# Gate weights two rows to a partition in four wide slots, down weights in four small ones

## Chip, cores and metric

The kernel runs on 1 core of a Trainium2 chip. The metric is the device time of one execution in microseconds, lower is better; the median of three runs is given. One further execution was taken by the profiler; its rows carry the readings below.

## What is computed

The reference is `second_block(first_block(x))` for 512 tokens of width 1024 in fp32. The first block is a gated convolution beside a linear recurrence, the second an attention layer (two kinds of heads) and a mixture of experts. The change touches the mixture of experts, which takes most of the time:

```python
def _moe_sequence(h, w_router, b_router, w_gate_up, b_gate_up, w_down, b_down):
    logits = (jnp.einsum('ld,de->le', h, w_router) + b_router).astype(jnp.float32)
    top_val, top_idx = lax.top_k(logits, TOP_K)
    gates = jax.nn.softmax(top_val, axis=-1).astype(h.dtype)
    ...
    xs = h[tok] 
    hgu = lax.ragged_dot(xs, w_gate_up, group_sizes) + b_gate_up[e_sorted]
    act = _clamped_swiglu(hgu)
    out = lax.ragged_dot(act, w_down, group_sizes) + b_down[e_sorted]
    out = out * gates.reshape(-1)[order][:, None]
    return jax.ops.segment_sum(out, tok, num_segments=L)
```

`w_gate_up` of one expert is 1024 x 2048 (8 MB), `w_down` 1024 x 1024 (4 MB). All 32 experts' weights are read once, 384 MB.

## The kernel before

The experts run as 32 passes, in the order of how many tokens chose them. A pass takes the expert's tokens in groups ("items") of up to 128; passes 3 and 9 (PAIRS) have two items, every other one has one, and what goes beyond is done by `further_tiles` (L1997). Weights come in pieces of 1 MB. `units(b)` (L298) lists what pass b consumes: 8 gate pieces of its own expert (128 rows of 2048 columns, one row to a partition, 8192 bytes) and then 4 down pieces of the expert before it (256 rows of 1024 columns; two neighbouring rows to a partition, 8192 bytes, or in the passes of PAIRS and TINY two rows 128 apart, 4096 bytes each).

The pieces go through `class Weights` (L89 to L160). `add` (L100) appends to a list of work, `issue` (L108) takes the next piece and the first free slot and starts one DMA on SyncE's queue (SP, L115), `release` (L148) gives a slot back and issues the next piece, and `get` hands the next piece over in order. There are 12 slots of 1 MB: 2 from the start (L221), 7 added at L1349, 3 at L2051. A DMA is issued at the moment in the program in which a slot is freed, so its place in SP's queue and the wait for the slot's last reader are set by that.

How a piece is used depends on the pass. In the passes called SMALL (1, 2, the even ones and the last six; few tokens) TensorE takes the piece in fp32 as it is (`small_products`, matmuls L1903, bias L1897), and the slot is released behind the piece's last matmul. In the others ScalarE and VectorE split it into a high and a low part (L140, L141), the slot is released there, and TensorE makes three products (L1921 for gates, L1932 for downs). In PAIRS the slot is kept until the second item has been through.

Beside the products of a pass, `beside(b)` lays out what prepares the next ones, by the index of the unit: ahead of unit 4 GpSimd gathers the rows of the next expert's tokens from DRAM (`rows_of`, an indirect DMA, L1569, on the software queue q0; weights are on q1), behind unit 9 TensorE transposes them (`transposed_rows` L1643 for small items of 64 or 32 rows, `transposed` L1648 for 128 rows), so that the contracted dimension lies on the partitions. The activations of the way down are transposed in `act_T` (L1673), which in passes with paired down rows reads every second column. A pass ends with a scatter that adds its rows to the result in DRAM (L1665, also on q0). Behind the last down piece stand the further tiles and the final layer norm (L2069 to L2160), which take four freed slots as scratch (`keep`).

Of the kernel before, what the change touches and what calls it, by code (L numbers as in the profile page):

```python
# [9 lines left out]
F32 = mybir.dt.float32  # L10
# [8 lines left out]
D = 1024  # L19
# [70 lines left out]
class Weights:  # L90
# [1 line left out]


    def __init__(self, nc, pools, slots):
        self.nc, self.slots = nc, list(slots)
# [4 lines left out]
    def add(self, *loads, split=True, n=2048, pieces=1, late=0):  # L100

        self.todo.append((loads, split, n, pieces, self.last + late))
        self.last += 1

    def ready(self):
        return self.raw and self.raw[0][-1] == self.used

    def issue(self):  # L108
        if not self.todo:
            return  # L110
        loads, split, n, pieces, at = self.todo.pop(0)
        pool, tag = slot = self.slots.pop(0)
        t = pool.tile([128, 2048], F32, tag=tag, name="wraw", bufs=1)
        for view, src in loads:
            self.nc.sync.dma_start(out=view(t), in_=src() if callable(src) else src)  # L115
        self.raw.append((t, split, n, pieces, slot, at))
        self.raw.sort(key=lambda r: r[-1])

    def prefetch(self):
        while self.slots and self.todo:  # L120
            self.issue()

    def split(self):
        t, s, n, pieces, slot, _ = self.raw.pop(0)
        self.used += 1
        if not s:
            self.part.append((t, slot))
            return
        raw = (t, slot)
        if s != "both":  # L130
            self.slots.append(slot)
        pool, tag = slot = self.parts.pop(0)
        self.parts.append(slot)
        hi = pool.tile([128, 2048], F32R, tag=tag + "h", name="whi", bufs=1)
        lo = pool.tile([128, 2048], F32R, tag=tag + "l", name="wlo", bufs=1)
        self.part.append((hi, lo, *raw) if s == "both" else (hi, lo))

        def piece(i):
            c = slice(n * i // pieces, n * (i + 1) // pieces)
            self.nc.scalar.copy(out=hi[:, c], in_=t[:, c])  # L140
            self.nc.vector.tensor_tensor(out=lo[:, c], in0=t[:, c], in1=hi[:, c].bitcast(F32), op=OP.subtract)  # L141
            if i == pieces - 1 and s != "both":
                self.issue()

        piece(0)
        self.rest = [lambda i=i: piece(i) for i in range(1, pieces)]

    def release(self, slot):  # L148
        self.slots.append(slot)
        self.issue()  # L150

    def ahead(self, n):
        while len(self.part) < n and self.ready():
# [15 lines left out]
def block_kernel(ctx, tc, A, out, dbg=None, upto=99):  # L169
# [48 lines left out]
        return t  # L218


    RAW, RAWK, RAWX = 2, 7, 3  # L221
    W = Weights(nc, wp, [(wp, f"wraw{i}") for i in range(RAW)])

    def flat(t):
        return t
# [60 lines left out]

    PASSES, ni = [], 0
    for p in range(NE):  # L290
        k = 1 + (p in PAIRS)
# [12 lines left out]
    def paired(p):  # L304

        return p not in PAIRS and p not in TINY

    def rows2(w, pairs):
        return w.rearrange("(p k) n -> p k n" if pairs else "(k p) n -> p k n", p=128)

    def add_unit(p, dn, u, of, late=0):
        def src():
            w = of(p)[dn]
            return rows2(w[256 * u:256 * u + 256, :], paired(p)) if dn else w[128 * u:128 * u + 128, :]
        W.add((kn(2, 1024) if dn else flat, src), split="both" if p in PAIRS else p not in SMALL,
              late=late)

    def add_block(b, of):
        for p, dn, u in units(b):
# [1026 lines left out]
    v_ = A["b_router_2"]  # L1346
    sp.dma_start(out=rb, in_=bass.AP(tensor=v_.tensor, offset=v_.offset, ap=[[0, 128], [1, NE]]))
    W.parts.insert(0, (pK, "wpart2"))
    W.slots += [(pK, f"wraw{RAW + i}") for i in range(RAWK)]  # L1349
    W.prefetch()  # L1350
    l1b = bcast(A["ln1_b_2"], pC, "l1b")
    xg2 = [pK.tile([128, D], F32, name=f"xg{i}") for i in range(2)]
# [269 lines left out]
    def pick(onehot_e, kt):  # L1622
# [373 lines left out]

    def further_tiles():  # L1997

        at_slot, slots = W.slots[0], W.slots[1:]
        total = nc.values_load(xt_i[0:1, NX:NX + 1], min_val=0, max_val=NX)  # L2000
        msch.close()
        with tc.For_i(0, total, 1) as it:  # L2002
            with tc.manual_schedule():
# [23 lines left out]
                for g, (w, src) in enumerate(((gu[:, 0:D], xT), (gu[:, D:], xT), (dn, aT))):  # L2027
                    p_ = [psa("pg") for _ in range(2)]
                    add_bias(p_, se, g, bias_p.bitcast(F32))
                    for q_ in range(4):  # L2030
                        wpool, tag = slots[nl % len(slots)]
                        nl += 1
                        t = wpool.tile([128, 2, 1024], F32, tag=tag, name="wl", bufs=1)
                        sp.dma_start(out=t, in_=rows2(w[256 * q_:256 * q_ + 256, :], g == 2))
                        for k in range(2):
                            for c in range(2):
                                pe.matmul(p_[c], src[:, 2 * q_ + k, :], t[:, k, 512 * c:512 * c + 512],
                                          start=False, stop=(q_ == 3 and k == 1))
                    if g < 2:
                        ac = pM.tile([128, 512], F32, tag="ac", name="ac", bufs=2)  # L2040
                        for c in range(2):
                            swiglu(p_[c].unsqueeze(1), ac[:, 256 * c:256 * c + 256], 1)
                        for c in range(2):
                            act.copy(out=aT[:, 4 * g + 2 * c:4 * g + 2 * c + 2, :], in_=act_T(ac, c))
                    else:
                        for c in range(2):
# [19 lines left out]
    for b in range(NE + 1):  # L2066
        before, midst = beside(b)
        for j, (p, dn, u) in enumerate(units(b)):
            j += 8 * (b == NE)  # L2069
            last = b == NE and u == 3  # L2070
            if last:
                keep = [slot for slot in W.slots if slot[0] is not pM][:4]
                for slot in keep:
                    W.slots.remove(slot)
                oT = keep[1][0].tile([128, 16, 128], F32R, tag=keep[1][1], name="oT", bufs=1)
                for i in range(4):
                    dve.tensor_scalar(out=oT[:, i, :], in0=iotab, scalar1=its[NI - 1]["tk"][:, i:i + 1], scalar2=None,
                                      op0=OP.is_equal)
                hx = []
                for p_, tag in keep[2:]:  # L2080
                    t = p_.tile([128, 2, D], F32, tag=tag, name="hx", bufs=1)
                    hx += [t[:, 0, :], t[:, 1, :]]
                l2 = keep[0][0].tile([128, 2, D], F32, tag=keep[0][1], name="l2", bufs=1)
                for k, v in enumerate((A["ln2_g_2"], A["ln2_b_2"])):
                    sp.dma_start(out=l2[:, k, :], in_=bass.AP(tensor=v.tensor, offset=v.offset, ap=[[0, 128], [1, D]]))
            run(before[j])
            if b == NE and u == 0:
                run([(finish, n) for n in PASSES[NE - 2]])
            if last:
                further_tiles()  # L2090
                for i in range(4):
                    sp.dma_start(out=hx[i], in_=acc_d[128 * i:128 * i + 128, :])
            ahead = AHEAD - (b == NE)
            w = W.get(ahead - 1)
            if len(PASSES[p]) > 1:
                n0, n1 = PASSES[p]
                products(n0, dn, u, w, lambda: None)
                run(midst[j])
                products(n1, dn, u, w, lambda: None)
            else:  # L2100
                products(PASSES[p][0], dn, u, w, lambda: run(midst[j]))
            if ahead > 1:
                W.beyond(3)
            else:
                W.ahead(ahead)
            if b == 0:
                next(ordering, None)
            elif b > 1:
                next(lists, None)
        if b == 0:  # L2110
            run(before[8])
# [75 lines left out]
```

## Time and profile before

| | |
|---|---|
| median of 3 runs | 1892.73 us (1892.15 to 1892.87) |
| profiled execution | 1887.72 us |
| its span | 1885.8 us, mean granted TensorE clock 0.962 |
| TensorE busy | 1701.9 us (90%) |
| VectorE, ScalarE, GpSimd busy | 1118.5, 751.9, 516.0 us |
| SP's DMA queue (q1) | 115568 packets, 475.24 MB, 63.7% of 16 engines over the span |
| GpSimd's DMA queue (q0) | 11024 packets, 25.39 MB, 4.9% |
| gate pieces | 256 DMAs of 1 MB, median 20.4 us from issue to landing |
| down pieces | 128 DMAs of 1 MB, median 21.5 us |

The span is the time between the first and the last instruction in the trace, the profiled execution's own time is the whole of it. Busy shares are averages over a kernel with unlike stages: the mixture of experts runs from about 809 to 1853 us of the span, and there the DMA engines are full most of the time. A line of a time slice or window gives each engine's busy time, TensorE's granted clock (1.00 is 2.4 GHz, 0.50 is 1.2 GHz) and the share of the 16 DMA engines; the share can read slightly above 1. In a timeline row the bracket at the end tells how long the engine was idle before it, and what ended that.

### The profile page before, as it was taken

What the parts mean: (1) busy time and instruction counts of PE and PEld (TensorE: products, weight loads), DVE (VectorE), ACT (ScalarE), POOL (GpSimd) and SP (SyncE); (2) the same over time, 40 slices, a digit from 0 to 9 for tenths busy, and PEclk for the clock granted to TensorE, in tenths of its full rate; (3) what the DMA queues carried; (4) which work ended last, traced back from release to release, by engine and by line L of the source; (5) the groups of instructions that cost most, each with busy time, mean ns of one, the idle gap of its engine ahead of it and who ended that gap; (6) DMA issues with size and microseconds to landing.
All of it is one profiled execution on the core that took longest, in us unless ns stands there. A gap on an engine that the chain in (4) does not pass through costs nothing. (4 is left out here: it accounts for less than half of the span.)

```text
span 1885.8 us, 23223 instructions
## 1 busy us (share of the span) xinstructions
PE 1701.9 (90%) x8713; PEld 1111.8 (59%) x8713; DVE 1118.5 (59%) x1425; ACT 751.9 (40%) x894; POOL 516.0 (27%) x400
## 2 busy tenths in 40 slices
PE   4899785979998899978999999999999999999885
PEld 3687664758787677854565565566446545642221
DVE  6799983785746555756665566557547645731013
ACT  5323532742335545332364344445435533520001
POOL 3899994550311221311121101111110101110102
PEclk8999897989999899989999999999999999999997
DMA  8322221336131003769999999999999999999993
GB/s 301 90 73 73 78 90 45 112 135 213 59 104 56 1 1 110 298 265 365 390 395 412 399 413 398 403 403 411 420 402 406 404 404 396 403 406 396 406 414 132
DMA packets 127442, 503.51 MB, mean 267 GB/s; under 512 B 15226, under 2 KB 57784, under 8 KB 79712
## 3 DMA queue, kind: packets, MB, share of 16 engines
q1 hardware_dynamic: 115568, 475.24, 63.7%
q0 software_dynamic: 11024, 25.39, 4.9%
q8 instruction: 69, 1.13, 0.2%
q10 hardware_dynamic: 736, 1.38, 0.2%
q14 instruction: 45, 0.37, 0.1%
HBM read 488.55 MB, written 19.84 MB: 270 GB/s over the span
## 5 line engine op out<-in xcount | busy, mean ns | idle before, releaser
L141 DVE TENSOR_TENSOR wlo<-wraw,whi 128x2048 fp32r<-128x2048 f32 (+1 forms) x201 | 457.0, 2282 | 152.9 <-ACT whi L140 146.7
L140 ACT CAST whi<-wraw 128x2048 fp32r<-128x2048 f32 (+1 forms) x201 | 379.6, 1891 | 193.6 <-DMA wraw<-w_down 73.8
L1903 PE MATMUL pg<-wraw,xTs 128*64 128x512 f32 (+1 forms) x1664 | 274.6, 516 | 12.0 <-DMA wraw<-w_gate_up 12.0
L1903 PEld LDWEIGHTS pg<-wraw,xTs 128*64 128x64 f32 (+1 forms) x1664 | 85.5, 126 | 169.1 <-issue 120.7
L1903 PE MATMUL pg<-wraw,ats 128*64 128x512 f32 (+1 forms) x832 | 145.0, 524 | 6.3 <-DMA wraw<-w_down 3.8
L1658 DVE TENSOR_SCALAR lp<-pg 128x512 f32<-128x512 f32 (+1 forms) x47 | 31.1, 662 | 198.4 <-ACT sg L1657 196.8
L1665 POOL DMA_INDIRECT acc_d<-y,back x20 | 34.2, 1711 | 381.4 <-ACT y L1875 363.9
L561 POOL TENSOR_TENSOR acc<-acc,sparel 128x512 f32<-128x512 f32 x91 | 133.3, 1464 | 7.7 <-ACT acc L550 0.2
L1569 POOL DMA_INDIRECT xg<-h_d,ix x34 | 53.8, 1583 | 247.2 <-PE pg L1903 115.9
L1921 PE MATMUL pg<-whi,xTh 128*128 128x512 f32 x416 | 116.2, 401 | 0.4 <-issue 0.4
L1921 PE MATMUL pg<-whi,xTl 128*128 128x512 f32 x416 | 114.8, 398 | 0.0
L1921 PE MATMUL pg<-wlo,xTh 128*128 128x512 f32 x416 | 113.2, 394 | 0.0
L1665 POOL DMA_INDIRECT acc_d<-y,ix x13 | 28.8, 2219 | 288.3 <-ACT y L1878 206.9
L554 DVE SCALAR_TENSOR_TENSOR pc<-v,C,pc 128x512 f32<-128x512 f32 x144 | 101.6, 748 | 2.1 <-ACT pc L550 0.9
L1657 ACT ACTIVATE sg<-pg 128x512 f32<-128x512 f32 (+1 forms) x47 | 25.7, 573 | 184.3 <-PE pg L1903 101.1
L559 POOL TENSOR_SCALAR sparel<-v,C 128x512 f32<-128x512 f32 x91 | 93.8, 1031 | 14.0 <-DVE V L476 5.4
L1921 PEld LDWEIGHTS pg<-whi,xTh 128*128 128x128 f32 x416 | 75.9, 188 | 26.0 <-issue 10.6
L1921 PEld LDWEIGHTS pg<-wlo,xTh 128*128 128x128 f32 x416 | 78.7, 189 | 17.7
L1903 PEld LDWEIGHTS pg<-wraw,ats 128*64 128x64 f32 (+1 forms) x832 | 40.8, 126 | 80.9 <-issue 52.4
L1921 PEld LDWEIGHTS pg<-whi,xTl 128*128 128x128 f32 x416 | 76.6, 188 | 16.3
L1932 PE MATMUL pg<-wlo,ath 128*128 128x512 f32 x208 | 67.9, 408 | 10.3 <-DVE wlo L141 10.3
L213 DVE TENSOR_TENSOR atl<-pat,ath 128x256 fp32r<-128x256 f32 x52 | 20.0, 421 | 92.4 <-ACT ath L212 92.4
(660 smaller groups left out, 3349.7 us busy)
## 6 DMA issues: line engine op xcount, KB each, us to landing
wraw<-w_gate_up SPq DMA_DIRECT2D x256, 1024.0 KB, 20.4
wraw<-w_down SPq DMA_DIRECT2D x128, 1024.0 KB, 21.5
wraw<-w_in SPq DMA_DIRECT2D x17, 1024.0 KB, 5.1
wraw<-w_out SPq DMA_DIRECT2D x8, 1024.0 KB, 4.9
mraw<-mod_w SPq DMA_DIRECT2D x7, 1024.0 KB, 15.4
wraw<-w_in SPq DMA_DIRECT2D x14, 512.0 KB, 4.1
wraw<-pw_w SPq DMA_DIRECT2D x4, 1024.0 KB, 5.1
wraw<-mod_w SPq DMA_DIRECT2D x4, 1024.0 KB, 5.1
```

The lines of the kernel that those rows point to most:

```text
L140: self.nc.scalar.copy(out=hi[:, c], in_=t[:, c])
L141: self.nc.vector.tensor_tensor(out=lo[:, c], in0=t[:, c], in1=hi[:, c].bitcast(F32), op=OP.subtract)
L554: dve.scalar_tensor_tensor(out=acc[:, c, :] if j == 29 and not np_ else st_["o"], in0=v[:, j:j + S], scalar=dw_col(j, c), in1=st_["o"], op ...
L559: pool.tensor_scalar(out=pr_, in0=v[:, j:j + S], scalar1=dw_col(j, c), scalar2=0.0, op0=OP.mult, op1=OP.add)
L561: pool.tensor_tensor(out=acc[:, c, :], in0=acc[:, c, :], in1=pr_, op=OP.add)
L1569: pool.indirect_dma_start(out=xg, out_offset=None, in_=h1_d[:, :], in_offset=bass.IndirectOffsetOnAxis(ap=ix[0:w], axis=0), bounds_check=S ...
L1657: act.activation(out=sg, in_=v2[:, :, :, 0], func=AF.Sigmoid, scale=1.702)
L1658: dve.tensor_scalar(out=lp, in0=v2[:, :, :, 1], scalar1=-6.0, scalar2=8.0, op0=OP.max, op1=OP.min)
L1665: pool.indirect_dma_start(out=dst, out_offset=bass.IndirectOffsetOnAxis(ap=ix, axis=0), in_=y, in_offset=None, bounds_check=nt * S - 1, oo ...
L1903: pe.matmul(o, l, t[:, c0:c0 + n_], start=False, stop=u == 3 and k == 1 if dn else u == 7)
L1921: pe.matmul(it["acc"][c // 2][:, c % 2, :], l, r[:, 512 * c:512 * c + 512], start=False, stop=u == 7 and j == 2)
L1932: pe.matmul(it["acc"][2][:, c, :], l, r[:, c0:c0 + 512], start=False, stop=end)
```

## The change

Gate units are added two at a time: one DMA of 2 MB brings 256 rows, rows 2p and 2p+1 of the block next to each other on partition p (16384 contiguous bytes). A list of slots for each size takes the place of the one list: four small slots of 1 MB (two from the start, one at L1349, one at L2051) serve the down pieces and all earlier weights, four wide slots of 2 MB (three at L1349, one at L2051) the gate pairs. The total is 12 MB as before. A wide slot carries two units, and only the second one gives it back; a released slot issues the next piece of its own size. The row order on the partitions makes unit 2i the even and unit 2i+1 the odd rows of a block, so the transpositions of the gathered tokens take every other column (`every_other`). The scratch of the tail is three wide slots in place of four, and `further_tiles` reads its down weights as neighbouring rows.

```diff
+    def add(self, *loads, split=True, n=2048, pieces=1, late=0, size=1):
+
+        self.todo.append((loads, split, n, pieces, self.last + late, size))
+        self.last += size
 
...
-    def issue(self):
-        if not self.todo:
-            return
-        loads, split, n, pieces, at = self.todo.pop(0)
-        pool, tag = slot = self.slots.pop(0)
-        t = pool.tile([128, 2048], F32, tag=tag, name="wraw", bufs=1)
+    def issue(self, *sizes):
+
+        for i, (loads, split, n, pieces, at, size) in enumerate(self.todo):
+            if size in sizes and self.slots[size]:
+                break
+        else:
+            return False
+        self.todo.pop(i)
+        pool, tag, _ = slot = self.slots[size].pop(0)
+        t = pool.tile([128, 2048 * size], F32, tag=tag, name="wraw", bufs=1)
         for view, src in loads:
             self.nc.sync.dma_start(out=view(t), in_=src() if callable(src) else src)
-        self.raw.append((t, split, n, pieces, slot, at))
+        for k in range(size):
+            self.raw.append((t[:, 2048 * k:2048 * k + 2048] if size > 1 else t, split, n, pieces,
+                             slot if k == size - 1 else (), at + k))
         self.raw.sort(key=lambda r: r[-1])
+        return True
 
     def prefetch(self):
-        while self.slots and self.todo:
-            self.issue()
+        while self.issue(1, 2):
+            pass
 
...
             if i == pieces - 1 and s != "both":
-                self.issue()
+                self.release(slot)
 
         piece(0)
         self.rest = [lambda i=i: piece(i) for i in range(1, pieces)]
 
     def release(self, slot):
-        self.slots.append(slot)
-        self.issue()
+        if slot:
+            self.slots[slot[2]].append(slot)
+            self.issue(slot[2])
 
...
         def src():
             w = of(p)[dn]
-            return rows2(w[256 * u:256 * u + 256, :], paired(p)) if dn else w[128 * u:128 * u + 128, :]
-        W.add((kn(2, 1024) if dn else flat, src), split="both" if p in PAIRS else p not in SMALL,
-              late=late)
+            if dn:
+                return rows2(w[256 * u:256 * u + 256, :], paired(p))
+            return w[128 * u:128 * u + 256, :].rearrange("(p k) n -> p (k n)", p=128)
+        if dn or u % 2 == 0:
+            W.add((kn(2, 1024) if dn else flat, src), split="both" if p in PAIRS else p not in SMALL,
+                  late=late, size=1 if dn else 2)
 
...
-    W.slots += [(pK, f"wraw{RAW + i}") for i in range(RAWK)]
+    W.slots[1].append((pK, "wraw2", 1))
+    W.slots[2] += [(pK, f"wide{i}", 2) for i in range(3)]
...
+    def every_other(k):
+
+        k0 = 256 * (k // 2)
+        return slice(k0 + k % 2, k0 + 256, 2)
+
     def transposed_rows(xg):
         w = xg.shape[0]
         pt = psa("pxt")
         for k in range(8):
-            pe.transpose(pt[:, w * k:w * k + w], xg[:, 128 * k:128 * k + 128], ident[0:w, 0:w])
+            pe.transpose(pt[:, w * k:w * k + w], xg[:, every_other(k)], ident[0:w, 0:w])
         return pt[:, 0:8 * w].rearrange("p (k n) -> p k n", k=8)
 
     def transposed(xg, a, pt):
         for k in range(4):
-            pe.transpose(pt[:, 128 * k:128 * k + 128], xg[:, 512 * a + 128 * k:512 * a + 128 * k + 128], ident)
+            pe.transpose(pt[:, 128 * k:128 * k + 128], xg[:, every_other(4 * a + k)], ident)
         return slice(4 * a, 4 * a + 4), pt.rearrange("p (k n) -> p k n", k=4)
 
...
-    W.slots += [(pM, f"wraw{RAW + RAWK + i}") for i in range(RAWX)]
+    W.slots[1].append((pM, "wraw3", 1))
+    W.slots[2].append((pM, "wide3", 2))
...
-                keep = [slot for slot in W.slots if slot[0] is not pM][:4]
+                keep = [slot for slot in W.slots[2] if slot[0] is not pM]
                 for slot in keep:
-                    W.slots.remove(slot)
-                oT = keep[1][0].tile([128, 16, 128], F32R, tag=keep[1][1], name="oT", bufs=1)
+                    W.slots[2].remove(slot)
+                oT = keep[0][0].tile([128, 16, 128], F32R, tag=keep[0][1], name="oT", bufs=1)
+                l2 = keep[2][0].tile([128, 2, D], F32, tag=keep[2][1], name="l2", bufs=1)
```

## Rows read from the trace of the kernel before

**Rows 1.** Windows: busy PE, PEld, DVE, ACT, POOL; PE clock, DMA share, GB/s.
```profile
950.00:1000.00 50.00, 49.86 (x382) 34.94 (x372) 34.16 (x31) 27.89 (x24) 8.45 (x4) 1.00 1.02 393
1750.00:1800.00 50.00, 42.47 (x190) 12.07 (x188) 3.68 (x13) 3.36 (x7) 3.72 (x4) 1.00 1.02 405
```
**Rows 2.** Waits of TensorE's weight loads, 1750 to 1850: total us, times, longest.
```profile
PEld pg L1903 <- DMA wraw<-w_gate_up: 22.6, 16, 3.0
```
**Rows 3.** The weight DMA issued at 939.7: issue ns, and us to landing.
```profile
L115 SPq DMA_DIRECT2D wraw<-w_down x1: 383/383/383, 939.7 to 939.7; - x1
DMA to landing us min/median/max: 5.0/5.0/5.0
```
**Rows 4.** The weight DMA issued at 1133.2, the same view.
```profile
L115 SPq DMA_DIRECT2D wraw<-w_gate_up x1: 333/333/333, 1133.2 to 1133.2; - x1
DMA to landing us min/median/max: 8.9/8.9/8.9
```
**Rows 5.** DMA in 877 to 880: packets; queue: packets, MB, share of 16.
```profile
DMA packets 331, 1.27 MB, mean 423 GB/s; under 512 B 21, under 2 KB 21, under 8 KB 331
q1 hardware_dynamic: 331, 1.27, 103.1%
```
**Rows 6.** DMA in 1197.5 to 1200, the same view.
```profile
DMA packets 147, 1.07 MB, mean 429 GB/s; under 512 B 16, under 2 KB 16, under 8 KB 16
q1 hardware_dynamic: 147, 1.07, 101.6%
```
**Rows 7.** All 34 gathers of L1569, from issue to landing.
```profile
DMA to landing us min/median/max: 3.4/9.0/11.4
```
**Rows 8.** DMA queues in 1017.5 to 1020, while a gather's rows move.
```profile
q1 hardware_dynamic: 102, 0.76, 72.1%
q0 software_dynamic: 97, 0.32, 31.1%
```
**Rows 9.** Timeline of TensorE: start, us, transposition, [idle before and what ended it].
```profile
843.35 0.68 PE L1643 MATMUL pxt<-sq,xg 32*128 32x32 f32 x8 [2.52 <-DMA xg<-h_d,ix]
865.49 0.68 PE L1643 MATMUL pxt<-sq,xg 64*128 64x64 f32 x8 [1.62 <-DMA xg<-h_d,ix]
895.40 0.82 PE L1648 MATMUL pxt<-sq,xg 128*128 128x128 f32 x5 [2.94 <-DMA xg<-h_d,ix]
...
964.12 1.03 PE L1648 MATMUL pxt<-sq,xg 128*128 128x128 f32 x8
999.34 0.71 PE L1643 MATMUL pxt<-sq,xg 64*128 64x64 f32 x8
1025.49 1.03 PE L1648 MATMUL pxt<-sq,xg 128*128 128x128 f32 x8
```
**Rows 10.** The gather issued at 953.2.
```profile
L1569 POOL DMA_INDIRECT xg<-h_d,ix x1: 1056/1056/1056, 953.2 to 953.2; - x1
DMA to landing us min/median/max: 9.6/9.6/9.6
```
**Rows 11.** The gather issued at 988.7.
```profile
L1569 POOL DMA_INDIRECT xg<-h_d,ix x1: 1904/1904/1904, 988.7 to 988.7; - x1
DMA to landing us min/median/max: 10.3/10.3/10.3
```
**Rows 12.** The gather issued at 1013.1.
```profile
L1569 POOL DMA_INDIRECT xg<-h_d,ix x1: 1063/1063/1063, 1013.1 to 1013.1; - x1
DMA to landing us min/median/max: 8.7/8.7/8.7
```
**Rows 13.** Windows behind two of these idle times, columns as in rows 1.
```profile
895.90:899.30 3.40, 3.40 (x28) 1.80 (x26) 3.40 (x5) 2.97 (x3) 0.00 (x0) 0.50 1.01 405
865.00:866.00 1.00, 0.51 (x8) 0.54 (x8) 1.00 (x1) 0.00 (x0) 0.00 (x0) 1.00 0.99 418
```
**Rows 14.** Weight loads of the transpositions: ns min/median/max, first and last start.
```profile
L1673 PEld LDWEIGHTS pat<-sq,ac x178: 137/198/222, 849.1 to 1835.1; 128*128 128x128 f32 x178
L1648 PEld LDWEIGHTS pxt<-sq,xg x104: 138/140/226, 814.3 to 1616.3; 128*128 128x128 f32 x104
```

More of the change, by code (lines that the diff above doesn't have):

```diff
@@ L94, in __init__ @@
     def __init__(self, nc, pools, slots):
-        self.nc, self.slots = nc, list(slots)
+        self.nc, self.slots = nc, {1: list(slots), 2: []}
         self.parts = [(pools, f"wpart{i}") for i in range(2)]
@@ L98, in __init__ @@
         self.last, self.used = 0, 0
-    def add(self, *loads, split=True, n=2048, pieces=1, late=0):
-        self.todo.append((loads, split, n, pieces, self.last + late))
-        self.last += 1
+    def add(self, *loads, split=True, n=2048, pieces=1, late=0, size=1):
+        self.todo.append((loads, split, n, pieces, self.last + late, size))
+        self.last += size
     def ready(self):
         return self.raw and self.raw[0][-1] == self.used
-    def issue(self):
-        if not self.todo:
-            return
-        loads, split, n, pieces, at = self.todo.pop(0)
-        pool, tag = slot = self.slots.pop(0)
-        t = pool.tile([128, 2048], F32, tag=tag, name="wraw", bufs=1)
+    def issue(self, *sizes):
[7 more added lines that the diff above has]
+        t = pool.tile([128, 2048 * size], F32, tag=tag, name="wraw", bufs=1)
         for view, src in loads:
             self.nc.sync.dma_start(out=view(t), in_=src() if callable(src) else src)
-        self.raw.append((t, split, n, pieces, slot, at))
+        for k in range(size):
+            self.raw.append((t[:, 2048 * k:2048 * k + 2048] if size > 1 else t, split, n, pieces,
+                             slot if k == size - 1 else (), at + k))
         self.raw.sort(key=lambda r: r[-1])
+        return True
     def prefetch(self):
-        while self.slots and self.todo:
-            self.issue()
+        while self.issue(1, 2):
+            pass
     def split(self):
@@ L129, in split @@
         raw = (t, slot)
-        if s != "both":
-            self.slots.append(slot)
-        pool, tag = slot = self.parts.pop(0)
-        self.parts.append(slot)
+        pool, tag = part = self.parts.pop(0)
+        self.parts.append(part)
         hi = pool.tile([128, 2048], F32R, tag=tag + "h", name="whi", bufs=1)
@@ L148, in release @@
     def release(self, slot):
-        self.slots.append(slot)
-        self.issue()
+        if slot:
+            self.slots[slot[2]].append(slot)
+            self.issue(slot[2])
     def ahead(self, n):
@@ L218, in bcast @@
         return t
-    RAW, RAWK, RAWX = 2, 7, 3
-    W = Weights(nc, wp, [(wp, f"wraw{i}") for i in range(RAW)])
+    W = Weights(nc, wp, [(wp, f"wraw{i}", 1) for i in range(2)])
     def flat(t):
@@ L1997, in further_tiles @@
     def further_tiles():
-        at_slot, slots = W.slots[0], W.slots[1:]
+        at_slot, *slots = W.slots[2] + W.slots[1]
         total = nc.values_load(xt_i[0:1, NX:NX + 1], min_val=0, max_val=NX)
@@ L2030, in further_tiles @@
                     for q_ in range(4):
-                        wpool, tag = slots[nl % len(slots)]
+                        wpool, tag, _ = slots[nl % len(slots)]
                         nl += 1
                         t = wpool.tile([128, 2, 1024], F32, tag=tag, name="wl", bufs=1)
-                        sp.dma_start(out=t, in_=rows2(w[256 * q_:256 * q_ + 256, :], g == 2))
+                        sp.dma_start(out=t, in_=rows2(w[256 * q_:256 * q_ + 256, :], True))
                         for k in range(2):
@@ L2078, in block_kernel @@
                                       op0=OP.is_equal)
[L2079 to L2083, printed above, removed]
+                t = keep[1][0].tile([128, 4, D], F32, tag=keep[1][1], name="hx", bufs=1)
+                hx = [t[:, i, :] for i in range(4)]
                 for k, v in enumerate((A["ln2_g_2"], A["ln2_b_2"])):
```

## The prediction

> **What bounds the kernel now.** I read first the windows by stage. In 950 to 1000 us TensorE is busy 49.86 of 50 us while the DMA share is full too; in 1750 to 1800 it is busy only 42.47 us with the DMA share still full [rows 1]. So one stage is set by TensorE's order and one by the transfers. The waits of TensorE's weight loads say the same of the end: from 1750 to 1850 they wait 22.6 us for gate pieces [rows 2].
>
> Next I looked for the point where the one hands over to the other, as a stall of TensorE moves the end only ahead of it. A gate piece lands 20.4 us after its issue in the median (the table above), as many stand ahead of it; the pieces issued at 939.7 and 1133.2 took 5.0 and 8.9 us [rows 3, 4]. There the queue had run (nearly) dry: SP had no slot to issue into until TensorE released one. A delay of TensorE before 1133 therefore shifts all later transfers by as much, and from 1133 on only the length of the transfers counts. The tail behind the last piece stays as it is.
>
> **Part 1, bigger packets (a gain after 1133).** A row of a piece is one packet on one of 16 DMA engines. In a window with only 4 KB weight packets, 3 us x 16 x 103.1% less 21 completion packets of 9 ns, over 310 packets, gives 159.0 ns each [rows 5]. In one with only 8 KB packets, 2.5 us x 16 x 101.6% less 16 x 9 ns, over 131, gives 309.1 ns [rows 6]. Two of 4 KB are 318.0: a packet carries 8.9 ns that do not depend on its size (the completion packets are priced at the same 9). One packet more or less at the windows' edges moves this by about 3, so 6 to 12. A 16 KB packet, which the trace does not show, should take 2 x 309.1 - 8.9 = 609 ns. A pair of gate units now costs each engine 16 packets and two completions; after, 8 and one: 9 x 9 = 81 ns less. Passes 11 to 31 have 21 x 4 = 84 pairs: **-6.8 us** (-4.5 to -9). In the stage before 1133 the same saving is worth nothing, because TensorE sets its time.
>
> **Part 2, slots.** The 12 MB, the order of use and the look-ahead are unchanged, but a wide slot comes free only after its second half, and TensorE may start on a first half only when 2 MB have landed. Where the queue is full neither shows, since the next piece has been waiting anyway. At 1133 it does: the last two gate units of that pass now go out as one pair into an almost dry queue, and land 5.0 + 2.4 us after the later one's issue (2.4 us is a second megabyte, 8 packets x 309 ns an engine) instead of 8.9 [rows 3, 4, 6]: **-1.5 us** (0 to -1.5). SP loses 128 of its issues of some 0.33 us [rows 4]; it waits for slots most of the time, so nothing. The start of the MoE stage and the tail get their data in the order of before: nothing.
>
> **Part 3, the gathers (a cost before 1133).** GpSimd's gather of an expert's tokens (L1569) shares the 16 engines with the weights. It lands 3.4 us after its issue at best, 9.0 in the median [rows 7]. In 1017.5 to 1020 the gather's queue sends 97 packets and the weights' 102, at a full share [rows 8]: one for one. A gathered row thus waits for one weight packet: 159 + 309 = 468 ns a row now, 159 + 609 = 768 with gate packets of 16 KB, +0.30. With 128 rows (8 an engine) that is +2.4 and with the first row +2.7 us; for 64 rows +1.4; for 32 rows +0.9. Who waits: TensorE already stands idle for a gather at 843.35 (2.52 us, 32 rows), 865.49 (1.62, 64 rows) and 895.40 (2.94, 128 rows) [rows 9]; there the whole of it counts, 0.9 + 1.4 + 2.7 = 5.0. The gather issued at 953.2 lands at 962.8, 1.3 us ahead of its transposition at 964.12; of its +2.7, 1.4 count (I take 1.3) [rows 9, 10]. The one of 988.7 lands at 999.0, 0.3 ahead of 999.34: +1.1 [rows 9, 11]. The one of 1013.1 lands 3.7 ahead of 1025.49: nothing [rows 9, 12]. Sum **+7.4 us**; bounds 0 (a row's wait stays as it is) and 16 more (rival B).
>
> **Part 4, TensorE's clock.** The idle of 2.94 us at 895.40 is followed by 3.4 us at a granted clock of 0.50, the 1.2 GHz level; the idle of 1.62 us before 865.49 is not, the clock there reads 1.00 [rows 9, 13]. That idle grows to about 3.0. If it then pays for such a stretch, half of 3.4 us is lost: **+1.7 us** (0 to 3.4).
>
> **Part 5, strided transpositions.** With rows 2p and 2p+1 on one partition, the x transpositions read every other column. Weight loads of L1673, which mostly read so already, take 198 ns against 140 in L1648 [rows 14]: 58 ns x 8 a group x 12 groups before 1133 (passes 0 to 9, two of them with two groups) = 5.6 us if nothing covers them. Loads overlap the matmul in front of them (PEld is a queue of its own), so 0 to 5.6; I take **+2.0**, nearer to covered.
>
> **Sum.** TensorE's stage +7.4 + 1.7 + 2.0 = +11.1; boundary and transfers -1.5 - 6.8 = -8.3; together +2.8 us. On the profiled execution that is 1887.72 + 2.8 = 1890.5. The median of the runs shown is 1892.73, 5.0 above that execution; the same +2.8 gives **1895.5 us**.
>
> **Rivals.**
> *A, faster: the gathers do not slow.* If engines share by bytes rather than one for one, or the transfers ahead of a gather thin out, part 3 and with it part 4 fall away: +2.0 - 8.3 = -6.3, 1886.4; with covered transpositions too -8.3, 1884.4. For it: the queue runs dry at times in this stage [rows 3]. Against it: 97 against 102 [rows 8].
>
> *B, slower: the wait ahead of a gather's first row doubles as well.* A 128-row gather needs 8 x 0.309 us more than an idle one for the weight packets between its rows; 9.0 - 3.4 - 2.5 leaves about 3 us, some nine packets of 309 ns, ahead of its first row [rows 6, 7]. If these are weight packets already queued in the engine, they become 16 KB packets too: +2.8 more at each of the five transpositions and +1.8 at 1025.49, where the slack is used up: +16 on top, **1911**. It decides from the point at which more than one weight packet stands between a gather's issue and its first row. For it: about 3 us that the alternation does not explain. Against it: row by row the trace alternates.
>
> The Trainium skill has a rule that speaks for B: "DMA: Bandwidth & Descriptors", section "Queues, rings and completion order", says that an engine drains a whole packet of typically 9 to 17 descriptors from one queue before it turns to the next. By that rule, an estimate, a gathered row would wait for 9 to 17 weight rows; the near-equal counts of the two queues disagree row by row [rows 8], while the unexplained 3 us would fit it once per gather.
>
> *C, same: the packets stay at 8 KB.* If the transfer is cut into 8 KB packets, there is no saving but the completion (-0.8) and no slower gather; with -1.5 at the boundary and +2.0 for the transpositions the sum is about -0.3, 1892.4. For it: no packet above 8 KB is in any window I read. Against it: the 4 KB and 8 KB packets follow the contiguous runs.
>
> The same page, section "Why small descriptors are slow (HBM only)", puts the fixed part of a packet at about 3 cycles, some 3.5 ns by its 850 MHz, an estimate; by it the gain of part 1 would be about 2.6 us and the total about 1900. The trace's 8.9 ns decides [rows 5, 6].
>
> **How the numbers follow.** About 0.2%, 3.8 us, is what a measurement of this kernel can tell from no change. Forecast 0.42: its centre is at +2.8, its own range by the small bounds 1889 to 1901; 0.02 of it counts as faster, 0.27 as same, 0.13 as slower. A 0.28, faster. B 0.15, slower. C 0.10, same. 0.05 for a slot that is released too late somewhere in TensorE's stage, slower. Faster 0.30, same 0.37, slower 0.33. The range runs from A's 1884 to 1906, where B's part beyond it leaves about 2 in 10 out.
>
> **What would show it.** After: weight packets of 16 KB near 609 ns; gathers that land in about 12 us, not 9.0; idle of TensorE for xg of about 3.4, 3.0 and 5.6 us near 843, 865 and 895, and new such idle at the next two; a stretch at 0.50 after 865; longer loads in L1648; a last stage some 7 us shorter from the dry point of pass 9 to the last piece. Gathers that stay at 9 us show A or C (the packets tell which), gathers of 14 us or more show B. The prediction is wrong if the last stage does not shorten, or if TensorE comes to wait for gate pieces before 1133.

## The result and the profile after

The changed kernel takes 1905.47 us (median, 1903.72 to 1910.31); beside it the kernel before takes 1892.44 (1886.62 to 1895.69). The ratio is 1.0077, interval 1.0061 to 1.0093: slower by 14.6 us, 11.5 to 17.6. The forecast was 1895.5, +2.8 us; 1905.47 still lies inside its range of 1884 to 1906, but by luck: the range ended there on account of rival B, and it was not B that came. The profiled executions are 1887.72 and 1904.7 us, +17.0.

TensorE's stage first: from the transposition of pass 0 to the one behind pass 9, the same work in both. Windows of before and then of after; the columns are those of [rows 1]:

```profile
814.60:1138.40 323.80, 306.93 (x2000) 185.89 (x1998) 192.43 (x231) 133.93 (x126) 38.16 (x23) 0.99 0.96 382
```
```profile
815.00:1155.50 340.50, 315.51 (x1999) 191.14 (x1997) 192.54 (x231) 133.85 (x126) 40.20 (x23) 0.96 0.93 366
```

The stage is 16.7 us longer: nearly the whole difference arises here. TensorE's idle time grows from 16.9 to 25.0 us (+8.1), its busy time by 8.6. The same transpositions as in [rows 9], in the timeline of TensorE after:

```profile
846.26 0.92 PE L1658 MATMUL pxt<-sq,xg 32*128 32x32 f32 x6 [4.94 <-DMA xg<-h_d,ix]
869.57 0.66 PE L1658 MATMUL pxt<-sq,xg 64*128 64x64 f32 x4 [1.71 <-DMA xg<-h_d,ix]
901.57 0.67 PE L1663 MATMUL pxt<-sq,xg 128*128 128x128 f32 x2 [4.59 <-DMA xg<-h_d,ix]
...
973.69 1.20 PE L1663 MATMUL pxt<-sq,xg 128*128 128x128 f32 x8 [0.45 <-DMA xg<-h_d,ix]
1013.48 0.83 PE L1658 MATMUL pxt<-sq,xg 64*128 64x64 f32 x5 [4.34 <-DMA xg<-h_d,ix]
1041.43 0.75 PE L1663 MATMUL pxt<-sq,xg 128*128 128x128 f32 x5
```

These waits are for gathers, and two are new. A third new one, of 1.44 us at 1106.77, takes the place of one of 1.51 in before, at 1093.97, that was for the split of tokens (xTl). All waits for gathers in the two windows sum to 7.1 us before and 17.5 after (+10.4); idle time for other reasons shrank by 2.3. The gathers of after, first all 34 (against [rows 7]), then the one behind 1013.48 (against [rows 11]):

```profile
DMA to landing us min/median/max: 3.3/10.6/14.9
...
L1579 POOL DMA_INDIRECT xg<-h_d,ix x1: 1908/1908/1908, 998.4 to 998.4; - x1
DMA to landing us min/median/max: 14.9/14.9/14.9
```

The busy time grew by the clock and by the strided transpositions. Windows of after behind the three long waits, and of before behind its first (its second stands in [rows 13]):

```profile
845.20:852.00 6.80, 5.74 (x28) 3.98 (x32) 1.02 (x2) 1.43 (x3) 0.00 (x0) 0.50 0.07 29
899.80:910.00 10.20, 8.43 (x62) 4.68 (x64) 9.07 (x10) 4.72 (x6) 0.00 (x0) 0.50 1.03 389
1012.50:1019.30 6.80, 5.82 (x52) 2.80 (x52) 0.17 (x1) 0.59 (x1) 0.00 (x0) 0.50 0.98 418
```
```profile
844.70:848.10 3.40, 3.40 (x18) 1.92 (x21) 1.15 (x2) 1.46 (x3) 0.00 (x0) 0.50 0.00 0
```

At 1.2 GHz TensorE is busy for 5.74 + 8.43 + 5.82 = 20.0 us after, against 3.4 + 3.4 before. If half of that were lost, it would be 10.0 against 3.4, +6.6, and 2.0 of the 8.6 would remain for the strides. The transpositions can be read by themselves, though. The same two windows, before and after, with the instructions that touch `pxt`, the tile that they write (busy PE, PEld, DVE, ACT):

```profile
814.60:1138.40 323.80, 10.69 (x97) 8.96 (x96) 6.51 (x10) 8.81 (x17) 0.99 0.96 382
```
```profile
815.00:1155.50 340.50, 14.67 (x96) 12.90 (x95) 6.51 (x10) 8.82 (x17) 0.96 0.93 366
```

They take 4.0 us more of TensorE, so that 4.6 are left for the clock: not all work lasts twice as long at 1.2 GHz. After, the strided transposition of 32 rows took 1.14 us for eight matmuls at 1110.67, at full clock, and 0.92 for six at 846.26, at half. Idle 8.1, clock 4.6, transpositions 4.0: 16.7.

The last stage gives nothing back. Two down pieces with 216 MB between them (the 152nd and the 368th MB of expert weights), in the view of the weight DMAs, before and then after:

```profile
L115 SPq DMA_DIRECT2D wraw<-w_down x1: 333/333/333, 1201.4 to 1201.4; - x1
DMA to landing us min/median/max: 18.0/18.0/18.0
...
L115 SPq DMA_DIRECT2D wraw<-w_down x1: 332/332/332, 1787.3 to 1787.3; - x1
DMA to landing us min/median/max: 21.0/21.0/21.0
```
```profile
L119 SPq DMA_DIRECT2D wraw<-w_down x1: 332/332/332, 1223.7 to 1223.7; - x1
DMA to landing us min/median/max: 12.8/12.8/12.8
...
L119 SPq DMA_DIRECT2D wraw<-w_down x1: 333/333/333, 1798.4 to 1798.4; - x1
DMA to landing us min/median/max: 26.7/26.7/26.7
```

They land 588.9 us apart before (1219.4 to 1808.3) and 588.6 after (1236.5 to 1825.1). Of 18 passes at 0.32 us, 5.8, some 0.3 came, and that is within the spread: in the profiles of the runs below that gather and scatter throughout, these 216 MB take 588.9 to 589.7 us with 8 KB packets (before, e1, e2, e3, e7, e8, e11) and 588.1 to 590.2 with 16 KB ones (after, e4, e5, e6).

### The profile page after: what moved, and what is told of

Read it like the earlier page. It is cut to its first block, busy times and chain, and to the rows that moved or that the text cites. A ratio compares the mean times of both kernels' runs of the same rounds, so it can differ in the third digit from the quotient of the medians.

```text
span 1902.9 us, 22682 instructions
## 1 busy us (share of the span) xinstructions
PE 1713.3 (90%) x8713; PEld 1126.1 (59%) x8713; DVE 1119.5 (59%) x1425; ACT 751.5 (39%) x894; POOL 504.6 (27%) x400
## 5 line engine op out<-in xcount | busy, mean ns | idle before, releaser
L1579 POOL DMA_INDIRECT xg<-h_d,ix x34 | 47.2, 1389 | 256.1 <-issue 102.2
L1680 POOL DMA_INDIRECT acc_d<-y,ix x13 | 23.9, 1838 | 268.4 <-ACT y L1893 125.6
L1947 PE MATMUL pg<-whi,ath 128*128 128x512 f32 x208 | 68.8, 412 | 0.0
```

The source lines that it names most:

```text
L1579: pool.indirect_dma_start(out=xg, out_offset=None, in_=h1_d[:, :], in_offset=bass.IndirectOffsetOnAxis(ap=ix[0:w], axis=0), bounds_check=S ...
L1680: pool.indirect_dma_start(out=dst, out_offset=bass.IndirectOffsetOnAxis(ap=ix, axis=0), in_=y, in_offset=None, bounds_check=nt * S - 1, oo ...
L1947: pe.matmul(it["acc"][2][:, c, :], l, r[:, c0:c0 + 512], start=False, stop=end)
```

## The experiments

Theories: **packets** (16 KB packets slow the gathers, TensorE idles and its clock falls), **slots** (a wide slot comes back, and a pair lands, too late), **strides** (the strided transpositions). All times are medians beside runs of the kernel before on the same chip; the us are the ratio times 1892. Executions of before spread over 1886 to 1901 us, so 2 us between two experiments is not a difference. One profile can also be shifted from its start: the first transposition of the expert stage stood between 814.1 and 820.2 us, which is why stretches are compared, not times of day.

**Four changes that take the edit apart.** e1 fills a wide slot with two transfers of 8 KB rows:

```diff
-            W.add((kn(2, 1024) if dn else flat, src), ...
+            W.add(*([(kn(2, 1024), src)] if dn else
+                    [(lambda t, k=k: t[:, 2048 * k:2048 * k + 2048], half(k)) for k in range(2)]), ...
```

> The changed kernel, but each wide slot is filled by two transfers, one with the even and one with the odd rows of its block, so that a packet is 8 KB again; slots, order and strided transpositions stay. Theory 'packets' (the 16 KB packets slow the gathers, TensorE idles for them and falls to half clock): gathers back at a median near 9.0 us from issue to landing, TensorE's waits for xg back near 7 us, time 1894 to 1898, which is before plus some 3 us for the strided transpositions. Rival 'slots' (a wide slot comes back too late): stays at 1903 or more. Rival 'strides' (the strided weight loads are what costs): stays at 1903 or more.

1897.87 us, ratio 1.0044 (1.0030 to 1.0057): +8.3, at the upper end of what packets allowed. Gathers are back at a median of 8.5 us. So the 16 KB packets cost some 6 us of the 14.6 (2 to 10 by the intervals), and of the 8 that stay theory packets had put only 3 down to the strides (4.0 by the transpositions above).

e2 keeps the wide slots but reads two blocks of 128 rows, so there are neither 16 KB packets nor strides:

```diff
-            return w[128 * u:128 * u + 256, :].rearrange("(p k) n -> p (k n)", p=128)
+            return w[128 * u:128 * u + 256, :].rearrange("(k p) n -> p k n", p=128)
...
-        k0 = 256 * (k // 2)
-        return slice(k0 + k % 2, k0 + 256, 2)
+        return slice(128 * k, 128 * k + 128)
```

> The changed kernel with wide slots of 2 MB, each filled by one transfer of two blocks of 128 rows, row 2i of one block and of the next on one partition: packets of 8 KB, no strided transposition. Packets: 1890 to 1894, the time of before, with gathers near 9.0 us. Slots: 1902 or more. Strides: also 1890 to 1894; e1 against this run is the price of the strides, about 3 us by theory packets and 12 or more by theory strides.

1901.46 us, ratio 1.0054 (1.0033 to 1.0074): +10.2, with gathers at 8.5 us. The slots alone are slower than before; theory packets misses this run by 8 us, and theory slots by 0.5. e1 less e2, named above as the price of the strides, is -1.9 us (about -6.6 to 2.8). The trace of e2 tells where the time goes. ScalarE's first cast of pass 3's weights in before, in e2 and in e1, and then TensorE in e2:

```profile
891.00 1.89 ACT L140 CAST whi<-wraw 128x2048 fp32r<-128x2048 f32 x1
```
```profile
897.36 1.90 ACT L145 CAST whi<-wraw 128x2048 fp32r<-128x2048 f32 x1 [5.45 <-DMA wraw<-w_gate_up]
```
```profile
900.03 1.89 ACT L145 CAST whi<-wraw 128x2048 fp32r<-128x2048 f32 x1
```
```profile
903.37 0.84 PE L1657 MATMUL pxt<-sq,xg 32*128 32x32 f32 x6 [3.95 <-DVE xTl L219]
```

Before, the piece is there when ScalarE comes to it. So it is in e1, which has the same wide slots but lets each half land by itself: the first half is issued at 888.5 and lands 11.3 us later, at 899.8, and TensorE's idle time in the stage is 16.0 us (in the slowest execution of e1, which is the one profiled), no more than before's 16.9 (e2: 20.1). In e2 the cast waits 5.45 us for the pair. Behind it in ScalarE's and VectorE's queues stands the split of the tokens, for which TensorE idles 3.95 us; the clock is at half from 902.3 to 912.5. It is then the landing of the pair as one transfer that costs idle time here; that a wide slot also comes back late shows no idle in e1. Where the delay comes from is in the issue of that first piece, in before and in after:

```profile
L115 SPq DMA_DIRECT2D wraw<-w_gate_up x1: 351/351/351, 877.7 to 877.7; - x1
DMA to landing us min/median/max: 11.6/11.6/11.6
```
```profile
L119 SPq DMA_DIRECT2D wraw<-w_gate_up x1: 350/350/350, 884.0 to 884.0; - x1
DMA to landing us min/median/max: 14.9/14.9/14.9
```

It lands at 889.3 before and at 898.9 after (897.3 in e2, issued 880.3): later issued, behind a queue that had itself restarted later (the first issue after the stretch in which the queue ran dry is at 850.5 before, 855.1 in e2, 857.2 after), and longer under way, with 2 MB to land. That the restart is late because a slot of two units is free only when both are consumed is read from the code; no run shows it by itself.

e3 puts only the row order and the strides into the kernel before:

```diff
-            return rows2(...) if dn else w[128 * u:128 * u + 128, :]
+            return rows2(...) if dn else \
+                w[256 * (u // 2):256 * (u // 2) + 256, :].rearrange("(p k) n -> p k n", p=128)[:, u % 2, :]
...
-            pe.transpose(pt[:, w * k:w * k + w], xg[:, 128 * k:128 * k + 128], ident[0:w, 0:w])
+            pe.transpose(pt[:, w * k:w * k + w], xg[:, every_other(k)], ident[0:w, 0:w])
```

> The kernel before with its 1 MB pieces and 12 slots, but each gate piece holds the even or the odd rows of a block of 256, and the transpositions of the tokens read every other column as in the change. Packets: before plus 2 to 4 us, since the steps of the transpositions of 64 and 32 rows went from 62 to 120 ns and those of 128 rows from 109 to 120. Strides: before plus 10 to 14. Slots: plus 0 to 4.

1897.04 us, ratio 1.0023 (1.0006 to 1.0040): +4.4 (1.1 to 7.6), just above what packets and slots allowed, and near the 4.0 us of the transpositions above. The three parts, +4.4, +10.2 and +6.3 (changed kernel against e1), sum to more than 14.6: they meet at the same place, pass 3, where gather and weights are late together, and each has 2 to 4 us of uncertainty.

e4 gathers earlier in the changed kernel:

```diff
-                before[4 + j].append((gather, n))
+                before[4 if j else 2].append((gather, n))
```

> The changed kernel with the gather for the next pass put ahead of unit 2 instead of unit 4, so some 5 to 10 us earlier. Packets: no idle of TensorE for xg at the later passes, no half-clock stretches behind them, 1885 to 1892: below before, since before's own waits of 7 us go too. Slots or strides: at most those 7 us go, 1897 to 1900.

1902.00 us, ratio 1.0061 (1.0037 to 1.0085): +11.5, so 3 us gained (the intervals allow none), not 14 or more. The waits at 870 and 901 shrink to 0.3 and nothing, and a new one takes their place:

```profile
904.76 0.93 PE L1658 MATMUL pxt<-sq,xg 32*128 32x32 f32 x6 [7.82 <-DVE xTl L219]
```

That is the same wait as in e2, behind the cast that waits for the pair. Both rivals had put this run within 1897 to 1900; it lies outside every forecast, nearer to theirs than to that of packets.

**The clock.** e5 fills the waits of the changed kernel with matmuls into a scratch bank:

```diff
     def xpose(n):
         it = its[n]
+        if n in (1, 2, 3, 7):
+            warm({1: 18, 2: 6, 3: 18, 7: 16}[n], bias_p)
```

> The changed kernel with 6 to 18 extra matmuls into a scratch bank ahead of the transpositions that wait longest for a gather (passes 1, 2, 3 and 6), so that TensorE works through most of the idle time. Nothing else moves. If half-clock stretches are what makes the idle dear: the granted clock stays at 1.00 through 844 to 1020 but for a stretch where TensorE waits for the split of tokens, and the time falls by 4 to 9 us against the changed kernel, to 1896 to 1901. If the idle alone counts: no gain, 1904 to 1907.

1899.85 us, ratio 1.0041 (1.0022 to 1.0059): 6.8 us faster than the changed kernel by the ratios (about 2 to 11), with more work. Windows of e5 over the two later stretches:

```profile
899.80:910.00 10.20, 10.20 (x98) 6.95 (x96) 9.74 (x11) 5.98 (x8) 1.64 (x1) 1.00 1.01 413
1012.50:1019.30 6.80, 6.80 (x33) 2.16 (x29) 0.76 (x2) 0.86 (x3) 1.56 (x1) 1.00 1.00 398
```

1.00 where after had 0.50; of the first stretch, 3.4 of its 6.8 us stay. The gathers were no faster (median 11.2 before 1130, as in after). So it is the half clock behind the idle, not the idle alone, that made these waits dear; 6.8 is near the 4.6 to 6.6 worked out above.

**Where the 16 KB packets cost.** e6 uses them from pass 11 on only, e1's transfers up to pass 10.

```diff
-                    [(lambda t, k=k: ..., half(k)) for k in range(2)]), ...
+            W.add(*([(kn(2, 1024) if dn else flat, src)] if dn or p > 10 else
+                    [(lambda t, k=k: ..., half(k)) for k in range(2)]), ...
```

> The changed kernel, with the wide slots filled by two transfers of 8 KB rows in passes 0 to 10 and by one of 16 KB from pass 11 on. Packets in TensorE's stage: the time of e1 or up to 2 us below it, 1895 to 1898, with gathers at 8.5 us before 1130 and at 10 after. If the 16 KB packets cost their time in the last stage: that of the changed kernel, 1903 to 1906. If they gain there what I forecast: 1890 to 1892.

1897.31 us, ratio 1.0021 (1.0008 to 1.0034): +4.0, so 10.6 below the changed kernel. The gathers of e6 up to 1130 and from 1140 on:

```profile
L1583 POOL DMA_INDIRECT xg<-h_d,ix x12: 928/1060/2810, 837.8 to 1127.9; - x12
DMA to landing us min/median/max: 7.6/8.9/10.3
...
L1583 POOL DMA_INDIRECT xg<-h_d,ix x21: 994/1001/2592, 1161.6 to 1793.8; - x21
DMA to landing us min/median/max: 8.6/10.5/13.7
```

In one kernel the gather takes 8.9 us beside 8 KB packets and 10.5 beside 16 KB ones. The cost of the packets is in TensorE's stage. What they gain behind it isn't seen in the trace: the same 216 MB take 589.7 us in e6. By the medians e6 is 4.3 us faster than e1 (about 1 to 8), from which it differs only by the larger packets behind pass 10; but its profile has no shorter last stage to show for it, and the five profiles with 16 KB packets behind pass 9 (after, e4, e5, e6, e12) take 747.4 to 750.3 us from the transposition behind it to the end, the seven with 8 KB ones 747.4 to 750.6.

**One piece less.** e7 gives before 11 slots (`RAW, RAWK, RAWX = 2, 7, 2`).

> The kernel before with 11 slots of 1 MB instead of 12. Slots (a wide slot that comes back after its second half is worth one piece of lead less, and the lead ahead of pass 3 has no slack): before plus 4 to 10 us, with the first gate piece of pass 3 landing after TensorE and ScalarE want it near 891, and idle of TensorE for xTl or weights there. If the lead has slack: within 2 us of before.

1898.64 us, ratio 1.0031 (1.0016 to 1.0047): +5.9. One megabyte of look-ahead is worth 3 to 9 us, so it has no slack. But not where I expected it: pass 3 is hardly touched (TensorE's wait for xTl there is 0.99 us), and the shift grows from 1.7 us at the transposition near 1061 to 6.0 at the one near 1144, where ScalarE's casts wait for late down pieces (7.08 us ahead of 1083, where before waits 5.31) and the last gates of pass 10 are issued at 1143.6 instead of 1133.2.

**Before with earlier gathers.** e8 is e4's edit on the kernel before. e11 keeps that, adds 10 warm matmuls at pass 1 and moves the transposition for pass 3 two units ahead.

> The kernel before with the gather for the next pass put ahead of unit 2 instead of unit 4. The idle at 865 and 895 (1.6 and 2.9 us) and the half-clock stretch at 895.9 go, that at 843 stays (its index is fetched only then): 3 to 6 us below before, 1886 to 1889. If the early gather only makes TensorE run into late weights at pass 3, as in e4: within 2 us of before.

> The kernel before with the gathers ahead of unit 2, the transposition for pass 3 two units earlier (so its split stands ahead of the cast that waits for the first weights of pass 3), and 10 extra matmuls in the wait at pass 1. If idle and half-clock stretches are what TensorE's stage can still give: the stretches at 844 and 895 go, 3 to 7 us below before, 1886 to 1890. If the weights' landing at pass 3 holds it anyway: within 2 us of before.

1894.84 us, ratio 1.0010 (0.9994 to 1.0025), and 1892.77, ratio 1.0012 (0.9999 to 1.0025): no gain, both forecasts of mine missed and the alternatives held. The wait for the gather is gone and another one comes a little later; TensorE in e8, and in e11:

```profile
898.86 0.84 PE L1643 MATMUL pxt<-sq,xg 32*128 32x32 f32 x6 [4.18 <-DVE xTl L213]
```
```profile
903.10 0.27 PE L1551 MATMUL pidx<-aux,oh 128*128 128x5 bf16 x4 [3.96 <-DVE oh L1540]
```

In e8 ScalarE's first cast of pass 3 waits 1.55 us for its piece, and the tokens' split stands behind that weights' split on VectorE. In e11 VectorE has no idle time from 894.6 until that matmul starts. So the start of pass 3 hangs on the landing and the splitting of its first weights as much as on the gather, in before too.

**The last stage without the rows.** e9 (before) and e10 (changed) leave out the gathers and scatters of passes 12 to 31:

```diff
-        it["ix"], it["xg"] = rows_of(it["pi"], small(n) or 1)
+        it["ix"], it["xg"] = rows_of(it["pi"], small(n) or 1, PASS_OF[n] > 11)
...
+            if PASS_OF[n] < 12:
+                scatter(y[:, c], it["ix"], small(n))
```

> The kernel before without the gathers and scatters of passes 12 to 31 (their tokens' rows are neither fetched nor added, so the sum over experts lacks these passes), so that the weights have the DMA engines to themselves there. In before, the 48 MB that land as pieces 321 to 368, all of passes with few tokens, take 127.4 us, 2.65 us a MB, where eight packets of 309 ns and a completion make 2.48. If the rows take the difference: some 119 us for these 48 MB. If something else does (a limit of the memory): 125 us or more.

> The same passes without gathers and scatters in the changed kernel, where these 48 MB take 127.7 us. If the larger packets save what I worked out (some 80 ns a pair) and the rows swallow it as long as they are there: 1.0 to 1.4 us less than e9 over these 48 MB, that is some 118. If the saving is not on the path at all: the same as e9 within 0.3 us.

1845.18 and 1876.99 us, of two runs each. The rows are what the weights lose in this stage, but TensorE becomes the bound before the DMA does, so it no longer waits for weights and the 48 MB of the expectations (120.6 us in e9, 121.7 in e10) don't measure the queue alone: e9 fits 'rows', but e10 against it did not answer what it was made for. Where the queue is full in both they compare. 1700 to 1780 us: the windows of e9 and e10, and the weight queue in each:

```profile
1700.00:1780.00 80.00, 80.00 (x378) 25.63 (x378) 9.16 (x25) 8.54 (x16) 0.00 (x0) 1.00 1.01 426
...
q1 hardware_dynamic: 4673, 34.01, 100.8%
```
```profile
1700.00:1780.00 80.00, 80.00 (x375) 27.99 (x375) 10.20 (x27) 8.27 (x15) 0.00 (x0) 1.00 1.01 426
...
q1 hardware_dynamic: 3092, 34.04, 100.6%
```

A third fewer packets, and 34.04 MB instead of 34.01. By my price (81 ns in every 3 MB, of some 7.4 us on an engine) it should have been 0.37 MB more. With the rows present, the same 80 us before and after:

```profile
q1 hardware_dynamic: 4328, 31.51, 96.1%
q0 software_dynamic: 521, 0.86, 4.7%
```
```profile
q1 hardware_dynamic: 2870, 31.31, 95.0%
q0 software_dynamic: 648, 1.10, 6.0%
```

32.4 MB of both queues together in either.

e10 is 31.8 us longer than e9, more than twice what the change costs with the rows. In the profiles 4.9 of them lie ahead of the first transposition of the experts, 19.5 in TensorE's stage (327.1 and 346.6 us), and 7.5 behind it. The stage up to pass 9 has all its rows in both runs, so it is a second look at the 16.7 above. Behind it TensorE sets the time in both, and there the transpositions alone account for the difference. The windows of e9 and e10 from the transposition behind pass 9 to the end, with the instructions that touch `pxt`:

```profile
1141.40:1844.20 702.80, 18.15 (x176) 15.45 (x176) 10.26 (x16) 16.52 (x30) 0.99 0.97 399
```
```profile
1165.80:1876.10 710.30, 25.28 (x176) 23.28 (x176) 10.26 (x16) 16.60 (x30) 0.99 0.96 395
```

7.1 of 7.5 us: where TensorE sets the time, the strided transpositions cost their full length.

**What is left when packets and clock are treated.** The wide slots and the strides stay. e12 is e6 with 14, 6 and 10 warm matmuls ahead of the transpositions of passes 1 to 3.

> e6 (8 KB packets in passes 0 to 10, 16 KB behind them, wide slots throughout) with 6 to 14 extra matmuls ahead of the transpositions of passes 1 to 3. In e6 the clock is at half for 6.8, 3.4 and 3.4 us behind these waits, 6.8 us lost in all. If the account closes that way: 4 to 7 us below e6, 1890 to 1894, equal to before. If the late landing of pass 3's first weights takes it back (as it took back the early gathers in e8 and e11): within 2 us of e6, 1895 to 1899.

1895.60 us, ratio 1.0016 (1.0004 to 1.0028): +3.0. In its trace the granted clock from 840 to 945 is 1.00, in e6 0.93; by the ratios it is 1 us below e6, which the intervals don't part from zero; the alternative (within 2 us of e6) held. No variant that does the whole work beats the kernel before.

## Why the forecast was wrong, step by step

Two steps failed outright: the 6.8 us that larger packets were to give back, of which nothing came, and the "nothing" for wide slots at the start of the stage, where a pair lands too late. The three costs that were forecast (gathers, clock, strides) came by the mechanisms given, each larger than its term.

- **Part 1, bigger packets: wrong in its result.** The price of a packet was right. A window of after with 16 KB packets alone (1762.5 to 1767.5):

```profile
DMA packets 148, 2.16 MB, mean 433 GB/s; under 512 B 16, under 2 KB 16, under 8 KB 16
q1 hardware_dynamic: 148, 2.16, 101.0%
```

  5 us x 16 x 101.0% less 16 x 9 ns over 132 is 611 ns; I had 609. But 7 ns less per packet in the records was not 7 ns on the engines: e9 and e10 move 426 GB/s alike, and the 216 MB took 588.9 and 588.6 us. By the prediction's own sign ("wrong if the last stage does not shorten") this alone refutes it. The failing step is "81 ns x 84 pairs", taken as time of the transfers. Shares above 100% say that neighbouring records overlap; that the fixed nanoseconds lie in that overlap is argued, not shown. By the Trainium skill, "DMA: Bandwidth & Descriptors", section "Why small descriptors are slow (HBM only)", a packet has a fixed overhead of about 3 cycles; at these sizes no run here shows it in the throughput.
- **Part 2, slots: wrong.** "Where the queue is full neither shows" and "the start of the stage ... nothing" left out the stretch from 850 to 940, where the queue has run dry just before and pass 3's first weights arrive as they are wanted (889.3 for a cast at 891.0). I had looked for waits of TensorE for weights and found none; the wait would have been ScalarE's, ahead of the split of the tokens. The prediction had given a slot that is released too late in this stage a chance of 0.05, but no cost; here it is the landing that costs. e2 prices it at +10.2 us (6.2 to 14), and e1, where each half lands by itself, has no such wait. At pass 9 the pair lands as forecast, 7.6 us after its issue (7.4 forecast),

```profile
L119 SPq DMA_DIRECT2D wraw<-w_gate_up x1: 332/332/332, 1150.3 to 1150.3; - x1
DMA to landing us min/median/max: 7.6/7.6/7.6
```

  at 1157.9, 15.8 behind before's 1142.1 where TensorE was 17.1 behind: 1.3 gained, 1.5 forecast. But it did not last: the 152nd MB lands 17.1 us behind before's again.
- **Part 3, gathers: right in mechanism, short in size, wrong in places.** Forecast +7.4 us of waiting for gathers; measured +10.4, of which 2.3 took the place of other idle time. Up to 1130 the median landing went from 9.0 to 11.2. But 865 got 0.1 instead of 1.4, and 843 and 999 got 2.4 and 4.3 instead of 0.9 and 1.1. The gather of 988.7 grew by 4.6 us where its 64 rows should have made 1.4. It stands on its queue behind a scatter issued 3.3 us before it, whose rows go between weight packets too: that scatter lands 9.8 us after its issue before and 14.0 after. The prediction counted only the gather's own rows. It also took the 97 and 102 packets of [rows 8] for rows; by the MB beside them (0.32 at 4 KB, 0.76 at 8 KB) some 77 and 93 are, the rest being completions, which is still near one for one. Rival B asked for 14 us as a rule and the median is 11.2; A and C are refuted by the gathers and the packets.
- **Part 4, clock: mechanism right, size off.** Forecast one more stretch of 3.4 us at half clock, +1.7. Measured +4.6 to 6.6: the stretches behind the longer waits were themselves longer (6.8 and 10.2 us) and a new one came at 1012.5. None came at 865, where I had put it. The lengths differ from one execution to the next: in e9, the same work up to pass 11, a third wait of 3.01 us is followed by 6.8 us at half where before's 2.94 had 3.4.
- **Part 5, strides: right in mechanism, half the size.** +2.0 forecast as "nearer to covered", 4.0 measured in the transpositions themselves, inside the bounds of 0 to 5.6. e3's +4.4 (1.1 to 7.6) fits that; e1 less e2 is too wide to say.
- **The sum.** In the profiled executions TensorE's stage gave +16.7 instead of +11.1, and everything behind it -0.1 instead of -8.3. The larger part of the miss is the gain that didn't come. "Slower by over 0.2%" had 0.33.

## What to carry to other kernels

Before a gain per packet is multiplied, look whether fewer packets move more bytes in a full window; here 34.01 and 34.04 MB did not differ. Merging two pieces into one transfer makes the first half land with the second (e2 against e1), and the place to look is where a queue has just run dry; ask which engine waits first there, not only whether the matmuls do. The long waits of TensorE (2.5 us and more in the rows of before and after) were paid twice here, once as idle and once at half clock, and filling them with matmuls got the second part back (6.8 us in e5). Transpositions that read every second column cost little only where TensorE does not set the time: 7.1 us between e9 and e10, nothing between before and after in the same passes.

## What was not expected of the hardware

- 8 KB and 16 KB packets move the same 426 GB/s when a queue has the engines to itself, though the records say 309 and 611 ns.
- A few gathered and scattered rows weigh much: without those of passes 12 to 31 the kernel before takes 47 us less, while in 1700 to 1780 us they are 0.86 MB of 32.4.
- The stretch at half clock is not of one length: 3.4 us behind idles of 2.52 and 2.94 us, 6.8 behind 4.94 and 4.34, and 10.2 where one of 4.59 stood close ahead of further waits. Nor does the idle time alone set it: 6.8 us follow one of 3.01 in e9, and 3.4 one of 1.32 in e3, while 1.62 in before and 1.71 in after have none.
